# A norm, a gate and the order of weight splits rearranged at the seams of a two-layer transformer

## The chip, the core and the metric

The program runs on one core of a Trainium2 chip. The metric is the device time of one execution in microseconds. TensorE multiplies matrices into PSUM, VectorE and ScalarE do elementwise work, GpSimd does a few odd operations, and the SyncE queue issues the loads. Each engine works through its own queue of instructions; where one needs the result of another, it waits.

## The reference

Two layers over 512 tokens of width 1024, all in fp32. Each layer mixes tokens, then runs a gated feed-forward block (hidden width 2816), each with a norm before and after and a residual.

```python
for layer in range(DEPTH):
    a = rmsnorm(h, ln_mix_pre[layer])
    mem_n = rmsnorm(mem, ln_mem[layer])
    if layer < N_A_LAYERS:
        proj = a @ w_in_a[layer]
        u, v, q_mem = ...
        main = chunked_spatial_gating(u, v, w_spatial[layer], ...)
    else:
        s_in = rmsnorm(h, ln_shared)
        kvf = s_in @ w_shared_kv
        k_s, v_s = ...
        log_f_s = jax.nn.log_sigmoid(kvf[..., 2 * MAIN_WIDTH:] + b_forget)
        proj = a @ w_in_b[layer - N_A_LAYERS]
        q, q_mem = ...
        main = forgetting_attention(q, k_s, v_s, log_f_s)
    mixed = jnp.concatenate([main, memory_attention(q_mem, mem_n, w_mem_kv[layer])], axis=-1)
    h = h + rmsnorm(mixed @ w_out[layer], ln_mix_post[layer])
    f = rmsnorm(h, ln_ffn_pre[layer])
    f = (jax.nn.silu(f @ w_ffn_gate[layer]) * (f @ w_ffn_up[layer])) @ w_ffn_down[layer]
    h = h + rmsnorm(f, ln_ffn_post[layer])
```

`forgetting_attention` adds the cumulative sum of `log_f_s` along the tokens to its logits, for twelve heads. `memory_attention` has four heads over 256 memory rows.

## The kernel before

**Numbers.** Every fp32 operand is cut into a high part, rounded by a ScalarE copy, and a low part, the rest, which VectorE subtracts (`split`, L240). A product is three matmuls (`mm3`, L191): high by high, high by low, low by high. A pair of weight parts lives in the tiles `whi` and `wlo`, eight buffers each. TensorE can start on `whi` as soon as ScalarE is done, and needs `wlo` at the third matmul.

**Stages.** Layer A: memory queries, value projection, memory heads, spatial gating. Then a feed-forward block, layer B (queries, keys, values, forget gates, four memory heads, twelve forgetting heads), and a second feed-forward block. Between them stands `boundary` (L835) three times: it finishes the tail of the one stage, transposes its rows into the hidden state `h`, adds up the squares for the next norm (`PairNorm`, L301) and runs the first four blocks of the next stage in halves of 256 tokens.

**Norms.** `finish` (L275) sums squares by a matmul against a column of 1/1024, one for each 128 tokens and each summed tile; `spread` (L292) lays the result over all partitions by `broadcast` (L249).

**The feed-forward block.** Hidden blocks are taken two at a time for the gate and the up projection. One such block of 256 hidden columns is a `Seven` (L921): seven products of twelve matmuls each, from sums of the quarters of the weight block, and from sums of the inputs made once (`combined`). `sums` (L940) makes the first sums (`s3` and some in place in `raw`) and splits the first two weights; `run` splits the others on their turn; `end` (L979) adds the seven results up into `s1` and `s2`, for which it reads PSUM after the last product (`a`), and hands the rows on to `gate_rows` (multiply by the norm `rbc`, then SiLU) or `up_rows` (multiply by the gate, then split into `fhi` and `flo`). The PSUM tiles of a Seven are `x`, `a` and `e`. `sevens` (L988) runs a gate Seven and an up Seven. For the first pair of a block it mixes the two; for the nine other pairs it runs them one after the other, products in the order 1, 7, 2, 6, 4, 3, 5. There are 20 Sevens in a block; after 6, 12 and 16 of them a down projection follows, and behind the last the tail. In this document Sevens are numbered as in the rows: odd ones are gates, even ones ups.

**What sets the order.** The code is written stage by stage, and a scheduler places each instruction in its engine's queue as its own estimates of readiness say, so that the queue of an engine can run ahead of the written order. `tc.issue_after(ins)` keeps instructions behind a given one on the same engine; it adds no wait between engines. Once built, the queues are fixed. Where stages meet, pieces of one stage are handed to another to fill TensorE (`fill`, `take`, `attend`).

**Forget gates.** Layer B loads the twelve columns `w_f`, splits them into one stationary tile of 24 columns and runs sixteen matmuls against the 512 tokens (L1185), turns the result with four transposes (L1190), and computes the log-sigmoid in small steps on VectorE and ScalarE (`az`, `e`, `l1`, `lf`). After six pieces of the value and key blocks it forms the cumulative sum with eight matmuls (`cs`, L1223). Only then do the memory heads start.

Of the kernel before, what the change touches and what calls it, by code (L numbers as in the profile page):

```python
# [40 lines left out]
def hybrid(ctx: ExitStack, tc: tile.TileContext, i: dict, out: bass.AP):  # L41
# [10 lines left out]
    last_load, last_exp = [None], [None]  # L52
# [80 lines left out]
    def pair_of_parts(n=512, aside=False):  # L133
        if aside:
            return act("whi"), act("wlo")
        return (wp.tile([P, 512], F32R, tag="hi", name=name("whi"), bufs=8)[:, :n],
                wp.tile([P, 512], F32R, tag="lo", name=name("wlo"), bufs=8)[:, :n])
# [102 lines left out]
    def split(src, hi, lo, eng=None):  # L240
        A.copy(hi, src)  # L241
        (eng or V).tensor_sub(lo, src, hi)  # L242

    def scaled_parts(src, g, hi, lo):

        A.activation(hi, src, AF.Copy, scale=g)
        V.scalar_tensor_tensor(out=lo, in0=src, scalar=g, in1=hi, op0=ALU.mult, op1=ALU.subtract)

    def broadcast(r4, tbs, o, c0):  # L249

        for tb in tbs:
            PE.matmul(o[:, tb * P - c0 : (tb + 1) * P - c0], r4[:, tb : tb + 1].to_broadcast([P, P]),
                      ident, start=True, stop=True)
# [47 lines left out]
    class PairNorm(Norm):  # L301
# [255 lines left out]
    def layer_a():  # L557
        a = parts("a")
        pre = Norm()
        wq, raws = ([], []), [wp.tile([P, 1024], F32, tag="raw", name=name("raw"), bufs=4) for _ in range(2)]  # L560
# [21 lines left out]
        vg = {}  # L582

        def value_block(j):

            w, o = [], []

            def load():
                for kh in range(2):
                    w.extend(prepared(i["w_a_v"][j, kh], (4, 256)))  # L590

            def piece(tk, kh):
                if kh == 0:
                    o.append(ps("mm", (P, 256), s="v"))
                c = slice(tk * P, (tk + 1) * P)
                for k in range(4 * kh, 4 * kh + 4):
                    mm3(o[tk], (a[k][0][:, c], a[k][1][:, c]), w[k], k == 0, k == KT - 1)
                if kh:
                    if tk % 2 == 0:
                        vg[j, tk // 2] = plain("vg", (P, 2, 256))  # L600
                    A.activation(vg[j, tk // 2][:, tk % 2, :], o[tk], AF.Copy, scale=pre.r4[:, tk : tk + 1])

            return load, [lambda tk=tk, kh=kh: piece(tk, kh) for tk in range(TB) for kh in range(2)]

        with tc.tile_pool(name="sgu", bufs=1) as lp:
# [8 lines left out]
            for f in take(fill, 1):  # L614
                f()
# [5 lines left out]
            for f in take(fill, 1):  # L621
                f()
            for cols in HALVES:
                pre.spread(cols, rbc)
# [4 lines left out]
            for f in take(fill, 3):  # L629
                f()  # L630
            xs = mem_inputs(0, memt)
            wk = mem_key_weights(0)
            for f in take(fill, 2):
                f()
            norm.finish((0, NMEM))
            for f in take(fill, 1):
                f()
# [197 lines left out]
    def boundary(phase, post, pre, nnorm, dst, block, evac, scaled=None):  # L835
# [5 lines left out]
        tail, ys = phase  # L841
        h0, h1 = HALVES
# [27 lines left out]
        for tb in range(3):  # L870
            tail(tb)
        turn(0, range(2))
# [48 lines left out]
    class Seven:  # L921
# [57 lines left out]
        def end(self):  # L979
            left, right = (slice(*c) for c in HALVES)  # L980
            s1, s2 = self.s1, self.s2
            V.tensor_add(s2[:, left], self.q, s2[:, left])
            V.tensor_add(s2[:, right], self.p, s2[:, right])  # L983
            self.rows(1, s2)
            V.tensor_add(s1, self.x, s1)
# [112 lines left out]
    def layer_b(phase, fp):  # L1098
# [51 lines left out]

        def value_block(j):

            w, o = [], []

            def load():
                for kh in range(2):
                    w.extend(prepared(i["w_v"][j, kh], (4, 256)))

            def piece(tk, kh):
                if kh == 0:  # L1160
                    o.append(ps("mm", (P, 256), s="v"))
# [3 lines left out]
                if kh:  # L1165
                    if tk % 2 == 0:
                        vals[j, tk // 2] = plain("vf", (P, 2, 256))
                    V.tensor_scalar_mul(vals[j, tk // 2][:, tk % 2, :], o[tk], r4b[:, tk : tk + 1])
# [5 lines left out]


        wf = wp.tile([P, KT, HEADS], F32, tag="wf", name="wf", bufs=1)
        wfs = wp.tile([P, KT, 2, HEADS], F32R, tag="wfs", name="wfs", bufs=1)
        later([(wf, i["w_f"])])
        split(wf, wfs[:, :, 0, :], wfs[:, :, 1, :])
        o = ps("mm", s="f")  # L1180
        n2 = 2 * HEADS
        for k in range(KT):
            w = wfs[:, k, :, :].rearrange("p a b -> p (a b)")
            for x in range(2):
                PE.matmul(o[:n2, :], w, s_act[k][x], start=(k, x) == (0, 0), stop=(k, x) == (KT - 1, 1))  # L1185
        zr = plain("zr")
        V.tensor_copy(zr[:n2, :], o[:n2, :])
        zt = ps("tr", (P, TB, 2, HEADS), s="zt")
        for tb in range(TB):
            PE.transpose(zt[:, tb, :, :].rearrange("p a b -> p (a b)"), zr[:n2, tb * P : (tb + 1) * P], ident[:n2, :n2])  # L1190
        bf = cp.tile([P, HEADS], F32, name="bf")
        later([(bf, i["b_f"].partition_broadcast(P))])

        def fsmall(s, dt=F32):
            return sp.tile([P, TB, HEADS], dt, tag="fs", name=name(s), bufs=10)

        z, zs = fsmall("z"), fsmall("zs")
        V.tensor_copy(zs, zt[:, :, 1, :])
        V.tensor_add(zs, zt[:, :, 0, :], zs)
        for tb in range(TB):  # L1200
            V.scalar_tensor_tensor(out=z[:, tb, :], in0=zs[:, tb, :], scalar=r4b[:, tb : tb + 1], in1=bf,
                                   op0=ALU.mult, op1=ALU.add)
        az, e, w1, l1, c1_ = fsmall("az"), fsmall("e"), fsmall("w1"), fsmall("l1"), fsmall("c1")
        A.activation(az, z, AF.Abs)
        A.activation(e, az, AF.Exp, scale=-1.0)

        V.tensor_scalar_add(w1, e, 1.0)
        A.activation(l1, w1, AF.Ln)
        V.scalar_tensor_tensor(out=c1_, in0=w1, scalar=-1.0, in1=e, op0=ALU.add, op1=ALU.subtract)
        V.reciprocal(w1, w1)  # L1210
        V.tensor_mul(c1_, c1_, w1)
        V.tensor_sub(l1, l1, c1_)
        lf = fsmall("lf")
        V.scalar_tensor_tensor(out=lf, in0=z, scalar=0.0, in1=l1, op0=ALU.min, op1=ALU.subtract)
        lfh, lfl = fsmall("lfh", F32R), fsmall("lfl", F32R)
        split(lf, lfh, lfl)
        for f in take(fill, 6):
            f()
        cs = ps("mm", s="cs")
        for tb in range(TB):  # L1220
            n = T - tb * P
            for part in (lfh, lfl):
                PE.matmul(cs[:HEADS, tb * P :], part[:, tb, :], tri[:, :n],  # L1223
                          start=(tb == 0 and part is lfh), stop=(tb == TB - 1 and part is lfl))
        cc = tp.tile([P, T], F32R, tag="acc", name="cc", bufs=2)
        ch, cl, nh, nl = (cc[32 * n : 32 * n + HEADS, :] for n in range(4))
        A.copy(ch, cs[:HEADS, :])
        V.tensor_sub(cl, cs[:HEADS, :], ch)
        A.activation(nh, ch, AF.Copy, scale=-1.0)
        V.tensor_sub(nl, ch, cs[:HEADS, :])  # L1230
# [13 lines left out]
        def head_parts(u, n):  # L1244
# [6 lines left out]
            for dst, src in ((qa[own, :], qh), (qa[other, :], ql), (ka[own, :], kh), (ka[other, :], kh),  # L1251
                             (qc[:64, :], qh), (kc[:64, :], kl)):
                nc.sync.dma_start(dst.bitcast(F32), src[own, :].bitcast(F32))
            nc.sync.dma_start(qc[66:68, :].bitcast(F32), cc[n : n + 33 : 32, :].bitcast(F32))
# [19 lines left out]
        between = {n: take(fill, c) for n, c in enumerate((3, 3, 4, 4, 4, 4, 4, 4, 3, 3, 3, 3))}  # L1274
# [103 lines left out]
```

## Time and profile before

| what | us |
|---|---|
| median of three timed runs (lowest, highest) | 1131.23 (1130.92, 1131.71) |
| span of the profiled execution | 1130.7 |
| TensorE busy | 1116.5 |
| weight loads busy | 1015.8 |
| VectorE busy | 893.1 |
| ScalarE busy | 662.2 |

The profile is one execution on the chip; the times in its rows count from the start of its span, and no separate device time stands for it beside the span. A row of the groups gives line, engine, operation, output<-inputs, shape and count, then busy time, mean ns of one, and the idle time ahead with what ended it. A row of the timeline gives start, duration, engine, line, operation, and in brackets the idle time ahead with what ended it; `x4` merges four neighbours. Matmuls are pipelined, so the sum of durations is more than the time between starts.

### The profile page before, as it was taken

The numbers are of one execution on the slowest core, as the hardware profiler recorded it, in microseconds if no ns is written. First come the engines' busy times: TensorE is split into PE (matmuls) and PEld (weight loads), VectorE is DVE, ScalarE is ACT, GpSimd is POOL, SyncE is SP. The second block draws the span as 40 slices with busy tenths as digits, with TensorE's granted clock in tenths as the row PEclk, the third lists the DMA queues.
The fourth block names the chain that finished last, engine by engine and source line by source line (L and its number), as shares of the span: only waits on it lengthen the run. The fifth ranks groups of instructions, "written<-read, shape, count | busy, mean of one in ns | idle before, by whom it ended". The sixth has DMA issues, their size and how long they took to land.

```text
span 1130.7 us, 19666 instructions
## 1 busy us (share of the span) xinstructions
PE 1116.5 (99%) x7470; PEld 1015.8 (90%) x7471; DVE 893.1 (79%) x1717; ACT 662.2 (59%) x1385; POOL 24.7 (2%) x42
## 2 busy tenths in 40 slices
PE   9999999999999999999999999999999999999997
PEld 6998889999899898998988898889999899898995
DVE  7878558897698587796858889958998688588775
ACT  8774468664365264476637667768765266254453
POOL 1000000000000000000000000000000000000000
PEclk9999999999999999999999999999999999999999
DMA  7513222334134223343323455521224234133222
GB/s 262 159 38 113 89 79 76 112 111 132 57 112 149 64 87 112 98 152 107 96 93 90 112 128 135 137 75 57 68 102 150 75 104 135 62 112 113 75 75 75
DMA packets 63559, 118.14 MB, mean 104 GB/s; under 512 B 5164, under 2 KB 39992, under 8 KB 63464
## 3 DMA queue, kind: packets, MB, share of 16 engines
q1 hardware_dynamic: 62584, 116.05, 33.1%
q8 instruction: 59, 0.97, 0.3%
q0 software_dynamic: 192, 0.52, 0.2%
q10 hardware_dynamic: 688, 0.31, 0.1%
q14 instruction: 36, 0.29, 0.1%
HBM read 104.71 MB, written 2.10 MB: 94 GB/s over the span
## 4 chain that ended last, share of the span: by engine, by line
PE 88%; DVE 4%; ACT 3%; issue 2%; DMA 2%; POOL 1%; SPq 0%; POOLq 0%; DVEq 0%
PE y L195 9%; PE y L194 9%; PE y L193 9%; PE a L195 5%; PE a L194 5%; PE a L193 5%; PE ps L193 4%; PE ps L195 4%; PE ps L194 4%; PE e L193 3%; PE e L195 3%; PE e L194 3%; PE x L195 3%; PE x L194 3%; PE x L193 3%
## 5 line engine op out<-in xcount | busy, mean ns | idle before, releaser
L241 ACT CAST whi<-raw 128x512 fp32r<-128x512 f32 x460 | 276.7, 620 | 271.4 <-PE y L195 111.3
L242 DVE TENSOR_TENSOR wlo<-raw,whi 128x512 fp32r<-128x512 f32 x460 | 305.6, 685 | 113.2 <-ACT whi L241 109.2
L193 PE MATMUL y<-whi,fhi 128*128 128x512 f32 (+1 forms) x356 | 138.5, 390 | 0.9 <-DVE s L983 0.6
L194 PE MATMUL y<-wlo,fhi 128*128 128x512 f32 (+1 forms) x356 | 138.0, 388 | 0.3 <-DVE wlo L242 0.3
L195 PE MATMUL y<-whi,flo 128*128 128x512 f32 (+1 forms) x356 | 138.1, 388 | 0.1
L193 PE MATMUL x<-xshi,whi 128*128 128x256 f32 x320 | 90.6, 283 | 0.0
L194 PE MATMUL x<-xslo,whi 128*128 128x256 f32 x320 | 90.6, 283 | 0.0
L195 PE MATMUL x<-xshi,wlo 128*128 128x256 f32 x320 | 90.6, 283 | 0.0
L194 PE MATMUL a<-xslo,whi 128*128 128x256 f32 x320 | 90.5, 283 | 0.0
L193 PE MATMUL a<-xshi,whi 128*128 128x256 f32 x320 | 90.5, 283 | 0.0
L195 PE MATMUL a<-xshi,wlo 128*128 128x256 f32 x320 | 90.4, 283 | 0.0
L193 PEld LDWEIGHTS y<-whi,fhi 128*128 128x128 f32 x356 | 66.9, 188 | 15.4 <-DVE s L983 1.3
L195 PEld LDWEIGHTS y<-whi,flo 128*128 128x128 f32 x356 | 66.9, 188 | 14.6 <-DVE flo L242 1.1
L194 PEld LDWEIGHTS y<-wlo,fhi 128*128 128x128 f32 x356 | 66.9, 188 | 14.3 <-DVE wlo L242 1.2
L193 PE MATMUL ps<-xshi,whi 128*128 128x256 f32 (+1 forms) x224 | 67.8, 305 | 0.0
L195 PE MATMUL ps<-xshi,wlo 128*128 128x256 f32 (+1 forms) x224 | 66.8, 300 | 0.0
L194 PE MATMUL ps<-xslo,whi 128*128 128x256 f32 (+1 forms) x224 | 66.2, 298 | 0.0
L193 PEld LDWEIGHTS a<-xshi,whi 128*128 128x128 f32 x320 | 61.4, 192 | 0.3
L194 PEld LDWEIGHTS a<-xslo,whi 128*128 128x128 f32 x320 | 61.4, 192 | 0.3
L193 PEld LDWEIGHTS x<-xshi,whi 128*128 128x128 f32 x320 | 61.4, 192 | 0.0
L194 PEld LDWEIGHTS x<-xslo,whi 128*128 128x128 f32 x320 | 61.4, 192 | 0.0
L195 PEld LDWEIGHTS x<-xshi,wlo 128*128 128x128 f32 x320 | 61.4, 192 | 0.0
(292 smaller groups left out, 3115.6 us busy)
## 6 DMA issues: line engine op xcount, KB each, us to landing
raw<-in_w_gate SPq DMA_DIRECT2D x44, 512.0 KB, 4.2
raw<-in_w_up SPq DMA_DIRECT2D x44, 512.0 KB, 3.5
raw<-in_w_down SPq DMA_DIRECT2D x44, 512.0 KB, 3.7
raw<-in_w_out SPq DMA_DIRECT2D x16, 512.0 KB, 4.7
raw<-in_w_b_q SPq DMA_DIRECT2D x8, 512.0 KB, 3.5
raw<-in_w_a_v SPq DMA_DIRECT2D x6, 512.0 KB, 6.4
raw<-in_w_a_u SPq DMA_DIRECT2D x6, 512.0 KB
raw<-in_w_v SPq DMA_DIRECT2D x6, 512.0 KB, 3.4
```

Source lines behind the costliest of these rows:

```text
L193: PE.matmul(o, w[0], x[0], start=start, stop=False, skip_group_check=more)
L194: PE.matmul(o, w[0], x[1], start=False, stop=False, skip_group_check=more)
L195: return PE.matmul(o, w[1], x[0], start=False, stop=stop, skip_group_check=more)
L241: A.copy(hi, src)
L242: (eng or V).tensor_sub(lo, src, hi)
```

## The change

It does these things. (1) `sevens` puts what `sums` issues on VectorE behind the last addition of the previous Seven. (2) `PairNorm` adds its two halves on VectorE and gives one tile to the sum by matmul instead of two. (3) `broadcast` uses a transpose instead of a matmul. (4) Layer A computes the squares of its norm behind the last split of its inputs, finishes the norm once for all tokens after three pieces of the value blocks, and holds back the copies of finished value pieces until the norm is there. (5) `boundary` puts the splits of the next stage's weights behind the first tail's, delays the last block by 3 steps instead of 4, and finishes the first half's norm after step 6. (6) The forget gates become twelve more columns of layer B's first value block: its weight tiles are 268 columns wide, and `z` is read from those columns. The log-sigmoid and the cumulative sum become pieces between the memory heads, which start without them; the counts of pieces between heads change to match.

```diff
+    @contextmanager
+    def behind(some):
+        with ExitStack() as s:
+            for ins in some:
+                s.enter_context(tc.issue_after(ins.ins))
+            yield
...
-            PE.matmul(o[:, tb * P - c0 : (tb + 1) * P - c0], r4[:, tb : tb + 1].to_broadcast([P, P]),
-                      ident, start=True, stop=True)
+            PE.transpose(o[:, tb * P - c0 : (tb + 1) * P - c0], r4[:, tb : tb + 1].to_broadcast([P, P]), ident)
...
+            t = self.sq[0, cols]
             if j:
-                V.tensor_add(self.sq[0, cols], self.sq[0, cols], self.sq[j, cols])
+                V.tensor_add(t, t, self.sq[j, cols])
+            if j == KT // 2 - 1:
+                V.tensor_add(t[:, 0, :], t[:, 0, :], t[:, 1, :])
         def sums(self, tb, cols):
-            c = slice(tb * P - cols[0], (tb + 1) * P - cols[0])
-            return [self.sq[0, cols][:, x, c] for x in range(2)]
+            return [self.sq[0, cols][:, 0, tb * P - cols[0] : (tb + 1) * P - cols[0]]]
...
-            for k in range(KT):
-                pre.add(h[:, k, :])
-            for cols in HALVES:
-                pre.finish(cols)
+            with behind(last_a):
+                for k in range(KT):
+                    pre.add(h[:, k, :])
+            pieces(3)
+            pre.finish(FULL)
+            pre.done = True
...
-        ws = [block(n) for n in range(4)]
-        outs = group(ws, inputs(0), h0, ["mm", "lg"] * 2, lag=4,
-                     after={3: lambda: turn(1, range(2)), 5: lambda: turn(1, range(2, 4))})
-        nnorm.finish(h0)
+        with behind(phase_parts):
+            ws = [block(n) for n in range(4)]
+        outs = group(ws, inputs(0), h0, ["mm", "lg"] * 2, lag=3,
+                     after={3: lambda: turn(1, range(2)), 5: lambda: turn(1, range(2, 4)),
+                            6: lambda: nnorm.finish(h0)})
...
-            V.tensor_add(s1, self.x, s1)
+            end = V.tensor_add(s1, self.x, s1)
             self.rows(0, s1)
+            ended[0] = end
+    ended = [None]
     def sevens(pair, plain_first):
         if not plain_first:
             for make in pair:
                 u = make()
-                u.sums()
+                with behind(ended):
+                    u.sums()
...
+            width = 256 + (0 if j else HEADS)
...
+                    raw = loaded(i["w_v"][j, kh]).rearrange("p (a b) -> p a b", b=256)
+                    for x in range(0, 4, 2):
+                        pair = [t.rearrange("p (a b) -> p a b", a=2) for t in pair_of_parts(2 * width)]
+                        k = 4 * kh + x
+                        split(raw[:, x : x + 2, :], *(t[:, :, :256] for t in pair))
+                        split(wf[:, k : k + 2, :], *(t[:, :, 256:] for t in pair))
...
+                    if j == 0:
+                        V.scalar_tensor_tensor(out=z[:, tk, :], in0=o[tk][:, 256:], scalar=r4b[:, tk : tk + 1], in1=bf,
+                                               op0=ALU.mult, op1=ALU.add)
...
-        split(wf, wfs[:, :, 0, :], wfs[:, :, 1, :])
-        o = ps("mm", s="f")
-        for k in range(KT):
-            w = wfs[:, k, :, :].rearrange("p a b -> p (a b)")
-            for x in range(2):
-                PE.matmul(o[:n2, :], w, s_act[k][x], start=(k, x) == (0, 0), stop=(k, x) == (KT - 1, 1))
...
-        between = {n: take(fill, c) for n, c in enumerate((3, 3, 4, 4, 4, 4, 4, 4, 3, 3, 3, 3))}
+        between = {n: take(fill, c) for n, c in enumerate((5, 5, 5, 5, 4, 4, 4, 4, 3, 3, 3, 3))}
+        between[1].insert(4, forget)
+        between[2].insert(3, cumulate)
```

The queues change most inside the feed-forward blocks. First VectorE around the end of Seven 7, in the first feed-forward block. In the rows the first number of a name counts the tile (`s2_7` is of Seven 7, `wlo_128` to `wlo_134` are the low parts of Seven 8, `wlo_135` and `wlo_136` of Seven 9), the second is a buffer number. Before:

```order
L982 TENSOR_TENSOR s2_7_3582<-e_7_3580,s2_7_3582 128x256
L242 TENSOR_TENSOR wlo_133_3809<-raw_53_3711,whi_133_3808 128x512
L242 TENSOR_TENSOR wlo_134_3825<-raw_54_3713,whi_134_3824 128x512
L242 TENSOR_TENSOR wlo_135_3866<-raw_55_3854,whi_135_3865 128x512
L983 TENSOR_TENSOR s2_7_3582<-a_7_3579,s2_7_3582 128x256
L985 TENSOR_TENSOR s1_7_3581<-x_7_3578,s1_7_3581 128x512
L1032 TENSOR_TENSOR s2_7_3582<-s2_7_3582,rbc_115 128x512
L1032 TENSOR_TENSOR s1_7_3581<-s1_7_3581,rbc_115 128x512
L242 TENSOR_TENSOR wlo_136_3871<-raw_55_3854,whi_136_3870 128x512
```

And with the change:

```order
L999 TENSOR_TENSOR s2_7_3574<-e_7_3572,s2_7_3574 128x256
L1000 TENSOR_TENSOR s2_7_3574<-a_7_3571,s2_7_3574 128x256
L1002 TENSOR_TENSOR s1_7_3573<-x_7_3570,s1_7_3573 128x512
L1053 TENSOR_TENSOR s2_7_3574<-s2_7_3574,rbc_115 128x512
L1053 TENSOR_TENSOR s1_7_3573<-s1_7_3573,rbc_115 128x512
L961 TENSOR_TENSOR s3_8_3712<-raw_53_3703,raw_54_3705 128x512
L241 TENSOR_TENSOR wlo_128_3715<-raw_53_3703,whi_128_3714 128x512
L963 TENSOR_TENSOR raw_54_3705<-raw_54_3705 128x512
L241 TENSOR_TENSOR wlo_129_3720<-raw_53_3703,whi_129_3719 128x512
L965 TENSOR_TENSOR raw_53_3703<-raw_54_3705,raw_53_3703 128x512
L241 TENSOR_TENSOR wlo_130_3739<-s3_8_3712,whi_130_3738 128x512
```

Before, all low parts of Seven 8 and the first of Seven 9 stood ahead of the addition `s2_7<-a_7`, which reads Seven 7's last product. Now that addition and the four instructions that follow from it stand ahead of Seven 8's first sum `s3_8` and its first low part `wlo_128`.

Second, TensorE where Seven 8 hands over to Seven 9. Before:

```order
L193 MATMUL a_8_3716<-xshi_6_2125,whi_134_3824 128x256
L194 MATMUL a_8_3716<-xslo_6_2126,whi_134_3824 128x256
L195 MATMUL a_8_3716<-xshi_6_2125,wlo_134_3825 128x256
L193 MATMUL a_9_3859<-xshi_1_1926,whi_135_3865 128x256
L194 MATMUL a_9_3859<-xslo_1_1927,whi_135_3865 128x256
L195 MATMUL a_9_3859<-xshi_1_1926,wlo_135_3866 128x256
```

And with the change:

```order
L193 MATMUL a_8_3708<-xshi_6_2132,whi_134_3816 128x256
L194 MATMUL a_8_3708<-xslo_6_2133,whi_134_3816 128x256
L195 MATMUL a_8_3708<-xshi_6_2132,wlo_134_3817 128x256
L193 MATMUL a_9_3851<-xshi_1_1920,whi_135_3857 128x256
L194 MATMUL a_9_3851<-xslo_1_1921,whi_135_3857 128x256
L193 MATMUL e_9_3852<-t3hi_1_2396,whi_137_3881 128x256
L195 MATMUL a_9_3851<-xshi_1_1920,wlo_135_3858 128x256
```

The first product of Seven 9 starts as before with the two matmuls on `whi_135`; one matmul of its second product (`e_9`) has moved ahead of the first one that needs `wlo_135`.

Third, ScalarE in layer B, around the forget gates (`az`, `e`, `l1`, `lfh`) and the memory heads' softmax (`mp`). Before:

```order
L1204 ACTIVATE az_1_6945<-z_1_6937 128x48
L1205 ACT_TABLE_LOAD
L1205 ACTIVATE e_21_6946<-az_1_6945 128x48
L1208 ACT_TABLE_LOAD
L1208 ACTIVATE l1_1_6948<-w1_1_6947 128x48
L241 CAST lfh_1_6960<-lf_1_6958 128x48
L241 CAST vals0_6872<-vf_1_7009 128x4x64
L241 CAST vals1_6873<-vf_1_7009 128x4x64
L1227 CAST cc_7083<-cs_1_7074 12x512
L1229 ACTIVATE cc_7083<-cc_7083 12x512
L432 ACT_TABLE_LOAD
L432 ACTIVATE mp_9_7128,sm_5_7097<-mlg_17_7129,nmx_5_7096 128x256
```

And with the change:

```order
L440 ACTIVATE mp_12_7135,sm_6_6912<-mlg_24_7158,nmx_6_6911 128x256
L1220 ACTIVATE az_1_7180<-z_1_6900 128x48
L241 CAST vals1_6863<-vf_2_7102 128x4x64
L1221 ACTIVATE e_21_7181<-az_1_7180 128x48
L241 CAST whi_283_7353<-q_11_6112 128x512
L1224 ACT_TABLE_LOAD
L1224 ACTIVATE l1_1_7183<-w1_1_7182 128x48
L241 CAST pT_21_7216<-tr_11_7215 128x512
L440 ACT_TABLE_LOAD
L440 ACTIVATE mp_13_7224,sm_7_6914<-mlg_25_7225,nmx_7_6913 128x256
```

Before, the chain and its table loads stood ahead of the first memory head's exponential (`mp_9`). Now two memory heads' exponentials come first, the chain stands between `mp_12` and `mp_13`, and two table loads with it.

More of the change, by code (lines that the diff above doesn't have):

```diff
@@ L1 @@
-from contextlib import ExitStack
+from contextlib import ExitStack, contextmanager
 import concourse.bass as bass
@@ L135, in pair_of_parts @@
             return act("whi"), act("wlo")
-        return (wp.tile([P, 512], F32R, tag="hi", name=name("whi"), bufs=8)[:, :n],
-                wp.tile([P, 512], F32R, tag="lo", name=name("wlo"), bufs=8)[:, :n])
+        return (wp.tile([P, max(n, 512)], F32R, tag="hi", name=name("whi"), bufs=8)[:, :n],
+                wp.tile([P, max(n, 512)], F32R, tag="lo", name=name("wlo"), bufs=8)[:, :n])
     def cut(pair, w):
@@ L559, in layer_a @@
         pre = Norm()
+        pre.done = False
         wq, raws = ([], []), [wp.tile([P, 1024], F32, tag="raw", name=name("raw"), bufs=4) for _ in range(2)]
@@ L613, in layer_a, with pieces @@
                         idle(2, zero, end)
-            for f in take(fill, 1):
-                f()
-            for k in range(KT):
-                pre.add(h[:, k, :])
-            for cols in HALVES:
-                pre.finish(cols)
+            def pieces(n):
+                for f in take(fill, n):
+                    f()
+            with behind(last_a):
[4 more added lines that the diff above has]
+            pre.done = True
             memt = load_mem()
[L621 to L624, printed above, removed]
+            pieces(1)
+            pre.spread(FULL, rbc)
             qf = [plain("q") for _ in range(2)]
@@ L628, in layer_a @@
             norm = mem_sums(memt)
-            for f in take(fill, 3):
-                f()
+            pieces(1)
             xs = mem_inputs(0, memt)
             wk = mem_key_weights(0)
-            for f in take(fill, 2):
-                f()
             norm.finish((0, NMEM))
-            for f in take(fill, 1):
-                f()
+            pieces(3)
             norm.spread((0, NMEM), rmem)
@@ L1186, in layer_b @@
[L1186 to L1228, printed above, removed]
@@ L1229, in layer_b, with forget @@
-        A.activation(nh, ch, AF.Copy, scale=-1.0)
-        V.tensor_sub(nl, ch, cs[:HEADS, :])
+        def forget():
+            az, e, w1, l1, c1_ = fsmall("az"), fsmall("e"), fsmall("w1"), fsmall("l1"), fsmall("c1")
+            A.activation(az, z, AF.Abs)
+            A.activation(e, az, AF.Exp, scale=-1.0)
+            V.tensor_scalar_add(w1, e, 1.0)
+            A.activation(l1, w1, AF.Ln)
+            V.scalar_tensor_tensor(out=c1_, in0=w1, scalar=-1.0, in1=e, op0=ALU.add, op1=ALU.subtract)
+            V.reciprocal(w1, w1)
+            V.tensor_mul(c1_, c1_, w1)
+            V.tensor_sub(l1, l1, c1_)
+            lf = fsmall("lf")
+            V.scalar_tensor_tensor(out=lf, in0=z, scalar=0.0, in1=l1, op0=ALU.min, op1=ALU.subtract)
+            sums["parts"] = fsmall("lfh", F32R), fsmall("lfl", F32R)
+            split(lf, *sums["parts"])
@@ new lines, in cumulate @@
+        def cumulate():
+            cs = ps("mm", s="cs")
+            lfh, lfl = sums["parts"]
+            for tb in range(TB):
+                n = T - tb * P
+                for part in (lfh, lfl):
+                    PE.matmul(cs[:HEADS, tb * P :], part[:, tb, :], tri[:, :n],
+                              start=(tb == 0 and part is lfh), stop=(tb == TB - 1 and part is lfl))
+            cc = sums["cc"] = tp.tile([P, T], F32R, tag="acc", name="cc", bufs=2)
+            ch, cl, nh, nl = (cc[32 * n : 32 * n + HEADS, :] for n in range(4))
+            A.copy(ch, cs[:HEADS, :])
+            V.tensor_sub(cl, cs[:HEADS, :], ch)
+            A.activation(nh, ch, AF.Copy, scale=-1.0)
+            V.tensor_sub(nl, ch, cs[:HEADS, :])
```

45 lines of the change are left out of this document (29 added, 16 removed).

## The prediction

> **What bounds the kernel now.** I read the busy shares first, then the chain that ended last, then the engines' waits, then one stretch of feed-forward work row by row.
>
> ```profile
> PE 1116.5 (99%) x7470; PEld 1015.8 (90%) x7471; DVE 893.1 (79%) x1717; ACT 662.2 (59%) x1385; POOL 24.7 (2%) x42
> ...
> PE 88%; DVE 4%; ACT 3%; issue 2%; DMA 2%; POOL 1%; SPq 0%; POOLq 0%; DVEq 0%
> ```
>
> TensorE is busy for 1116.5 of 1130.7 us and carries 88% of the chain: what leaves TensorE's queue is gained in full, and what makes it wait is lost in full. VectorE's 79% is an average; in the feed-forward blocks it looks different:
>
> ```profile
> 320.00:340.00 20.00, 20.00 (x169) 20.00 (x168) 19.17 (x34) 12.62 (x26) 0.00 (x0) 1.00 0.32 106
> ```
>
> Columns are the stretch, its length, then busy time of PE, PEld, DVE, ACT and POOL, granted clock and DMA. In these 20 us TensorE never stops and VectorE is busy for 19.17. Two engines run side by side, each with about as much work as there is time. That holds only while VectorE prepares the next Seven's weights during the present Seven's products. An edit that puts the two one behind the other shows at once.
>
> **The change part by part.** The diff has three kinds of edits, and they pull in opposite directions.
>
> *Less work on TensorE.* Four stretches give the prices:
>
> ```profile
> 183.50 0.95 PE L284 MATMUL st<-avg,sq 128*128 128x1 f32 x8
> 184.32 0.36 PE L193 MATMUL ps<-xshi,whi 128*128 128x256 f32 x1
> ...
> 185.86 0.71 PE L252 MATMUL rb<-ident,r 128*128 128x128 f32 x4
> 186.33 0.36 PE L195 MATMUL ps<-xshi,wlo 128*128 128x256 f32 x1
> ```
>
> Four norm sums leave eight records and hold the queue from 183.50 to 184.32, 0.82 us. At the three boundaries each half now sends two sums instead of four: six times 0.41, 2.5 us. Two broadcasts leave four records and hold it from 185.86 to 186.33, 0.47 us, two records each; as transposes I count one record each, which is how the attention's transposes stand in the groups (64 records for 64 tiles):
>
> ```profile
> L448 PE MATMUL tr<-ident,mp 128*128 128x128 f32 x64 | 9.1, 272 | 0.0
> ```
>
> Half of 0.47, for ten pairs of broadcasts: 2.4 us. [...]
>
> ```profile
> 584.92 0.40 PE L1185 MATMUL f<-shi,wfs 128*24 128x512 f32 x1
> ...
> 588.61 0.28 PE L193 MATMUL v<-whi,shi 128*128 128x256 f32 x1
> ...
> 589.65 0.42 PE L1190 MATMUL zt<-ident,zr 24*128 24x24 f32 x4
> 590.00 0.39 PE L195 MATMUL v<-whi,slo 128*128 128x256 f32 x1
> ```
>
> The forget gates' sixteen matmuls hold the queue for 3.69 us and their four transposes for 0.35. Against them stand twelve more columns in 96 matmuls. From 0.23 us between starts at 512 columns (rows L1185) and 0.12 at 256 (rows at 309 us, below), a column costs 0.43 ns: 96 x 12 x 0.43 ns = 0.5 us. Net 3.5 us. Together the three leave TensorE 8.4 us less.
>
> *Moves around seams.* Layer A's squares go behind the splits of its inputs, its norm is finished once, boundaries run with lag 3 and finish after step 6, and the forget chain goes between memory heads. What could be won is bounded by TensorE's waits at such places, of which the largest are
>
> ```profile
> PE yt L799 <- ACT y L792: 1.4, 3, 0.6
> PE idle L88 <- DVE zeros L80: 1.3, 1, 1.3
> PE mlg L465 <- ACT mp L432: 1.0, 1, 1.0
> PE rb L252 <- POOL r L256: 0.9, 2, 0.7
> ```
>
> (total, times, longest). Some 2 us of it (rb and mlg) is in reach. What could be lost is two ACT table loads, now between softmaxes of the second and third memory head:
>
> ```profile
> L1208 ACT ACT_TABLE_LOAD x1 | 1.3, 1283 | 0.0
> ```
>
> twice 1.28 us, with key-block matmuls on TensorE as cover; without it up to 2.6 us. I take these moves at 0, with ends of -2 and +3 us. New VectorE adds for the norms (six of 256 columns, 0.33 us apart at the boundaries) stay off TensorE's path, since they replace sums that come later anyway.
>
> *The order inside the Sevens.* This is the large term. `sums()` of a Seven is put behind the previous Seven's last addition on VectorE. VectorE takes its queue in order. The previous Seven's end needs its last product; the next Seven's first product needs, at its third matmul, `wlo`, which now stands behind that end. Before, `wlo` was written a whole Seven earlier. So TensorE and VectorE wait for each other once per Seven. The rows for the price, first the hand-over:
>
> ```profile
> 309.06 0.28 PE L195 MATMUL e<-t,wlo 128*128 128x256 f32 x1
> 309.18 0.28 PE L193 MATMUL x<-xshi,whi 128*128 128x256 f32 x1
> ...
> 309.45 0.42 DVE L982 TENSOR_TENSOR s<-e,s 128x256 f32<-128x256 f32 x1 [0.24 <-PE e L195]
> ```
>
> Matmuls start 0.12 us apart; the last one ends 0.28 after its start; VectorE begins 0.11 after that end. Call that end E. Then VectorE's pitch:
>
> ```profile
> 323.49 0.42 DVE L983 TENSOR_TENSOR s<-a,s 128x256 f32<-128x256 f32 x1
> 323.82 0.68 DVE L985 TENSOR_TENSOR s<-x,s 128x512 f32<-128x512 f32 x1
> 324.42 0.68 DVE L1038 SCALAR_TENSOR_TENSOR s<-s,s 128x512 f32<-128x512 f32 x1
> 325.02 0.68 DVE L1040 TENSOR_TENSOR s<-s,s 128x512 f32<-128x512 f32 x1
> 325.62 0.68 DVE L242 TENSOR_TENSOR wlo<-raw,whi 128x512 fp32r<-128x512 f32 x1
> ```
>
> Starts are 0.60 to 0.61 apart at 512 columns, and each is done 0.68 after its start. ScalarE's copy, which `s1` needs, takes 0.37:
>
> ```profile
> 322.75 0.37 ACT L971 COPY s<-a 128x256 f32<-128x256 f32 x1
> ```
>
> Gate to up: `s2` at E+0.11, `s1` after the copy at E+0.51, two products with `rbc` at 1.12 and 1.72, the sum `s3` at 2.33, `wlo` at 2.93, done at 3.62. With 0.10 for the hand-over to TensorE (a guess of mine near the 0.11 above), the third matmul starts at E+3.72 instead of E+0.08: a wait of 3.64. The second product's third matmul comes twelve matmuls (1.44) later, at 5.16, but its `wlo` stands four instructions on, done at 6.04, started at 6.14: 0.98 more. After that each product (1.44) outlasts one or two instructions of VectorE. Together 4.62 us.
>
> Up to gate: five instructions of 512 columns stand ahead of `wlo` instead of four (`flo` of the hidden block is among them), so it is done at E+4.22; the first wait is 4.12. Then five more stand ahead of the second product's `wlo`, done at 7.25, with thirteen matmuls of cover: 1.47. Together 5.59 us.
>
> How often: each layer has Sevens 1 to 20. The first two overlap as before, and 7, 13 and 17 begin behind a down projection, whose matmuls cover the preparation. Fifteen hand-overs are bare in a layer, nine gate to up and six up to gate, thirty in the kernel. One of them, ahead of Seven 19 in the first layer, also has eight memory inputs between its low parts:
>
> ```profile
> 27.36 2.46 DVE L247 SCALAR_TENSOR_TENSOR mparts<-mem,gains,mparts 128x256 fp32r<-128x256 f32 x6
> ```
>
> 0.41 each, 3.3 us, of which some 2.1 shows. 18 x 4.62 + 12 x 5.59 + 2.1 = 152.3 us.
>
> *Sum.* 1130.7 - 8.4 + 152.3 = 1274.6 us of span; the median run, 1131.23, stands 0.5 above the profiled span, so 1275.
>
> **The rivals.** *The clock falls in the gaps.* So far no wait is above 1.3 us, and the granted clock is 1.00 throughout. The gaps would be 3.6 and 4.1 us, thirty times. The trace shows TensorE after an idle start:
>
> ```profile
> 6.52 0.50 PE L194 MATMUL ps<-alo,whi 128*128 128x512 f32 x1 [0.29 <-DVE alo L247]
> ...
> 7.55 0.50 PE L193 MATMUL ps<-ahi,whi 128*128 128x512 f32 x1
> 7.89 0.40 PE L194 MATMUL ps<-alo,whi 128*128 128x512 f32 x1
> 8.27 0.50 PE L195 MATMUL ps<-ahi,wlo 128*128 128x512 f32 x1
> ...
> 9.87 0.39 PE L195 MATMUL ps<-ahi,wlo 128*128 128x512 f32 x1
> 10.10 0.40 PE L193 MATMUL ps<-ahi,whi 128*128 128x512 f32 x1
> ```
>
> After the last wait that the view notes, at 6.52, matmuls start 0.34 to 0.38 us apart, and from 9.87 on 0.23: a slow spell of 3.4 us. A spell of that length at half pace loses 1.7 us; about 1.0 of it is covered, since the slow first product hides the second wait. That leaves 0.7 us for each of thirty gaps; a spell twice as long would leave 2.4. So 1296 to 1347, in the middle 1320. [...]
>
> *Only the first wait shows.* If ScalarE and VectorE regain the second product's parts in the first gap, the 0.98 and 1.47 fall away: 35 us less, 1240. Against it: VectorE's rows have no idle time in between to regain.
>
> *Faster after all.* The end of a Seven would have to reach VectorE before TensorE needs the low part, which takes 3.7 us of matmuls after E that need no low part, thirty of them; the new order has two or three (0.24 to 0.36). If the queue order were not kept on the chip, the sum would be 1130.7 - 8.4 + 0.5: 1123. The trace of before keeps the built order row for row there, so I give this little.
>
> **How the numbers follow.** Forecast 1275: 0.67. Clock rival 0.20, first wait alone 0.08, faster 0.04, no difference 0.01 (within 0.2%, about what a measurement can tell here). The hand-over, 0.11 either way for sixty waits, and the moves at -2 and +3 bound the forecast's own range to 1262 to 1290. The range given, 1250 to 1325, reaches up to the middle of the clock rival; it leaves out that rival's upper part (0.06) and the cases below (0.13).
>
> **What would show it.** VectorE: `s<-a` of L1000 idle behind PE at each Seven, then `wlo` late; TensorE: waits of some 3.7 and 1 us on `wlo` of DVE, in total about 150, all in the feed-forward slices; its busy time down by about 8 us if the clock holds, and 256-column matmuls 0.12 apart right after a gap. If they stand 0.24 apart there, the clock rival holds. If layer B's forget term is wrong, its stretch is not 3 us shorter. The forecast is wrong if VectorE's wait at the end of a Seven is short.

## The result, and the profile after

The changed kernel takes 1313.41 us (median of four runs, 1311.67 to 1315.5) beside 1131.31 us for the kernel before: a ratio of 1.161, 95% interval 1.159 to 1.162. The time lies in the range given, 38 us above the predicted one. The first lines of the page of after, with the line of the granted clock, PEclk (one digit for each fortieth of the span, in tenths of TensorE's full clock):

```profile
span 1310.1 us, 19297 instructions
PE 1183.6 (90%) x7408; PEld 1066.3 (81%) x7409; DVE 891.4 (68%) x1721; ACT 660.7 (50%) x1388; POOL 25.4 (2%) x41
PEclk9999999789888989979999999999889889979989
```

TensorE has 62 matmul records fewer than before and is busy 67 us longer; it now also stands still for some 126 us. A smaller amount of work that takes longer means that it ran slower: the clock line is not all nines any more, and the mean granted clock fell from 0.999 to 0.937. In the trace it stands at 1.00 or at 0.50. At 0.50 for a share s of the span the mean is 1 - s/2, so s is 12.6%, some 165 us.

Where TensorE waits (total us, times, longest), and where VectorE does:

```profile
PE a L195 <- DVE wlo L241: 66.9, 21, 3.7
PE e L193 <- ACT whi L241: 45.6, 12, 4.1
PE e L195 <- DVE wlo L241: 2.0, 4, 0.6
PE x L195 <- DVE wlo L241: 1.8, 1, 1.8
```

```profile
DVE s L999 <- PE e L195: 138.2, 38, 6.2
DVE s L1000 <- ACT s L988: 83.5, 33, 2.8
```

Three of the 21 waits on `wlo` last 0.17 us; the other 18 are the gate-to-up hand-overs. The 12 in the second row are those from up to gate, where TensorE waits for the `whi` of the second product, which ScalarE copies from VectorE's sum `s3`. Together 30 long waits, 112 us. VectorE in turn waits 222 us at the end of a Seven for its last products (L999) and for ScalarE's copy of the last one (L1000), at places where it worked on the next weights before. At each bare hand-over the two engines now wait for each other.

One hand-over in order of time (start, duration, engine, instruction, idle time before it), on VectorE and on TensorE:

```profile
338.18 0.42 DVE L1000 TENSOR_TENSOR s<-a,s 128x256 f32<-128x256 f32 x1 [2.77 <-ACT s L988]
338.52 0.68 DVE L1002 TENSOR_TENSOR s<-x,s 128x512 f32<-128x512 f32 x1
339.11 1.28 DVE L1053 TENSOR_TENSOR s<-s,rbc 128x512 f32<-128x512 f32 x2
340.31 0.69 DVE L961 TENSOR_TENSOR s<-raw,raw 128x512 f32<-128x512 f32 x1
340.92 0.68 DVE L241 TENSOR_TENSOR wlo<-raw,whi 128x512 fp32r<-128x512 f32 x1
```

```profile
337.69 0.28 PE L194 MATMUL a<-xslo,whi 128*128 128x256 f32 x1
341.66 0.58 PE L195 MATMUL a<-xshi,wlo 128*128 128x256 f32 x1 [3.69 <-DVE wlo L241]
...
343.32 0.42 PE L193 MATMUL a<-xshi,whi 128*128 128x256 f32 x1
343.53 0.41 PE L194 MATMUL a<-xslo,whi 128*128 128x256 f32 x1
...
348.16 0.28 PE L194 MATMUL x<-xslo,whi 128*128 128x256 f32 x1
348.28 0.28 PE L195 MATMUL x<-xshi,wlo 128*128 128x256 f32 x1
```

VectorE runs through exactly the instructions that the prediction counted, and the wait is 3.69 us. It starts on them later than counted: `s<-a` (L1000) comes behind ScalarE's copy of the same product, 0.45 us after that product's end at 337.73, where the prediction had 0.11. What follows is the new part: matmuls start 0.21 us apart, and only from 347.5 on 0.12.

### The profile page after: what moved, and what is told of

It is laid out like the page before. It is cut to its first block, busy times and chain, and to the rows that moved or that the text cites. A ratio compares the mean times of both kernels' runs of the same rounds, so it can differ in the third digit from the quotient of the medians.

```text
span 1310.1 us, 19297 instructions
## 1 busy us (share of the span) xinstructions
PE 1183.6 (90%) x7408; PEld 1066.3 (81%) x7409; DVE 891.4 (68%) x1721; ACT 660.7 (50%) x1388; POOL 25.4 (2%) x41
## 4 chain that ended last, share of the span: by engine, by line
PE 78%; DVE 13%; ACT 5%; issue 3%; DMA 1%; POOL 1%; SPq 0%; POOLq 0%; DVEq 0%; ACTq 0%
PE y L193 8%; PE y L194 8%; PE y L195 8%; PE a L195 5%; PE a L193 4%; PE a L194 4%; PE e L195 4%; PE e L193 4%; PE e L194 3%; PE x L193 3%; PE x L195 3%; PE x L194 3%; PE ps L195 3%; PE ps L193 3%; PE ps L194 3%
## 5 line engine op out<-in xcount | busy, mean ns | idle before, releaser
L195 PE MATMUL a<-xshi,wlo 128*128 128x256 f32 x320 | 107.9, 337 | 66.9 <-DVE wlo L241 66.9
L195 PEld LDWEIGHTS a<-xshi,wlo 128*128 128x128 f32 x320 | 73.3, 229 | 73.5 <-DVE wlo L241 73.5
L999 DVE TENSOR_TENSOR s<-e,s 128x256 f32<-128x256 f32 x40 | 17.0, 424 | 138.2 <-PE e L195 138.2
L194 PE MATMUL a<-xslo,whi 128*128 128x256 f32 x320 | 100.2, 313 | 0.0
L193 PE MATMUL e<-t3hi,whi 128*128 128x256 f32 x160 | 58.9, 368 | 45.6 <-ACT whi L241 45.6
L193 PE MATMUL a<-xshi,whi 128*128 128x256 f32 x320 | 100.0, 312 | 0.0
L193 PEld LDWEIGHTS e<-t3hi,whi 128*128 128x128 f32 x160 | 43.5, 272 | 48.1 <-ACT whi L241 48.1
L988 ACT COPY s<-a 128x256 f32<-128x256 f32 x40 | 14.8, 370 | 117.6 <-PE a L195 117.6
L1000 DVE TENSOR_TENSOR s<-a,s 128x256 f32<-128x256 f32 x40 | 16.9, 423 | 83.5 <-ACT s L988 83.5
L194 PEld LDWEIGHTS a<-xslo,whi 128*128 128x128 f32 x320 | 70.9, 222 | 0.3
```

The source lines that it names most:

```text
L193: PE.matmul(o, w[0], x[0], start=start, stop=False, skip_group_check=more)
L194: PE.matmul(o, w[0], x[1], start=False, stop=False, skip_group_check=more)
L195: return PE.matmul(o, w[1], x[0], start=False, stop=stop, skip_group_check=more)
L988: A.copy(s1[:, right], self.p)
```

## The experiments

**One edit undone, and that edit alone.** The first kernel takes the order inside the Sevens back and keeps the rest of the change; the second adds only that order to the kernel before.

```diff
-                with behind(ended):
-                    u.sums()
+                u.sums()
```

> The changed kernel with one edit taken back: sums() of a Seven is no longer put behind the previous Seven's last addition; all other edits stay. Theory (the order inside the Sevens is the whole loss): the thirty waits on wlo and the half clock go with it; granted clock 1.00, and the time is 1131.3 - 8.4 = 1123 us, 1120 to 1126 with the moves at -2 and +3. Rival (the other edits lose too, at the seams or in layer B): 1131 us or more, with new waits of TensorE outside the feed-forward blocks.

> The kernel before with that one edit alone: sums() behind the previous Seven's last addition. Theory: the whole loss stands here again, 1313.4 - 1123 = 190 us over the kernel before, so 1322 us, 1316 to 1327, with a mean granted clock near 0.94 and thirty waits of 3.7 us. Rival (part of the loss needs the other edits beside it): under 1310 us. The forecast as it was made, without a fall of the clock: 1131.3 + 152.3 = 1284 us.

Measured: 1123.19 us without it, ratio to before 0.9928 (0.9916 to 0.9941), and 1329.12 us with it alone, ratio 1.174 (1.173 to 1.176). A line of the page of the first, and the waits of the second:

```profile
PE 1108.6 (99%) x7409; PEld 1003.3 (89%) x7409; DVE 893.2 (80%) x1721; ACT 659.4 (59%) x1388; POOL 25.4 (2%) x41
```

```profile
PE a L195 <- DVE wlo L242: 66.5, 19, 3.7
PE e L193 <- ACT whi L241: 45.5, 12, 4.1
```

The whole loss is this one edit; all others together are a gain. Alone it costs 198 us, 8 more than within the change (190), outside what was expected: the waits are the same to 0.5 us, but the mean clock is 0.927 and not 0.937. The gaps lie elsewhere in time there, and more of that kernel runs at half clock.

**The gaps filled.** The next kernel separates waiting from the clock. It adds matmuls that nobody reads, behind the last product before each of the thirty bare hand-overs:

```diff
                 u = make()
+                if end_mm[0] is not None:
+                    idle(12, tri, end_mm[0])
                 with behind(ended):
```

> The changed kernel with twelve more matmuls of 512 columns, whose result nobody reads, behind the last product before each of the thirty bare hand-overs: 12 x 0.23 = 2.8 us of work in a gap of 3.7 us. Theory (of the loss, 112 us are the first waits and some 71 us are matmuls at half clock after the gaps): the clock stays at 1.00, TensorE starts at full pace after each gap, and now waits for the second product as forecast, 0.98 or 1.47 us: 1270 to 1280 us, with more work in the kernel than the changed one. Rival (the matmuls after a gap are slow for a reason other than the gap, such as VectorE working beside them): 1313 us or more. Rival (the second wait doesn't come): near 1240 us.

Measured: 1254.66 us (1253.94 to 1255.15). More work, and 59 us less time: that is the price of the half clock, as far as the filling changes nothing else. Its waits, and the start of a Seven behind the filling:

```profile
PE a L195 <- DVE wlo L241: 17.1, 18, 1.0
PE e L193 <- ACT whi L241: 12.8, 12, 1.4
PE x L195 <- DVE wlo L241: 3.3, 1, 3.3
```

```profile
330.22 2.89 PE L88 MATMUL idle<-tri 128*128 128x512 f32 x12
332.95 0.28 PE L193 MATMUL a<-xshi,whi 128*128 128x256 f32 x1
333.07 0.28 PE L194 MATMUL a<-xslo,whi 128*128 128x256 f32 x1
334.31 0.38 PE L195 MATMUL a<-xshi,wlo 128*128 128x256 f32 x1 [0.96 <-DVE wlo L241]
334.53 0.28 PE L193 MATMUL a<-xshi,whi 128*128 128x256 f32 x1
...
335.81 0.28 PE L193 MATMUL x<-xshi,whi 128*128 128x256 f32 x1
...
336.76 0.33 PE L195 MATMUL e<-t3hi,wlo 128*128 128x256 f32 x1
```

The filling takes 2.7 us and 0.96 is left to wait: the same hand-over of 3.7 us, now at full clock (one gap of the thirty still ends in slow matmuls, 0.41 us each from 234.11 to 237.10), and VectorE works beside the matmuls as in the changed kernel: from 320 to 380 us it is busy for 37.9 us at a granted clock of 1.00, there for 32.9 at 0.86. So here it is the gap that makes them slow, not VectorE's work beside them. The time is below the 1270 to 1280 expected, since the second wait hardly shows: in this kernel's order TensorE does eight matmuls of `x` between the parts of `e` that need no low part and the one that does (335.81 to 336.76).

**How much idle time the clock stands.** Two more kernels fill each gap with six and with eight matmuls.

> The changed kernel with six filling matmuls in each of the thirty gaps in place of twelve: 1.4 us of work, so that some 2.3 us of each gap stay idle, and no stretch of 3.41 us is without a matmul. Theory (the clock is set on a grid of 3.41 us; it falls after a stretch in which TensorE was busy for less than about 1.6 us, whatever the idle time was made of): an idle run of 2.3 us brings a stretch under 1.6 us when it lies so on the grid that 1.8 us of it or more fall into one stretch, in some 60% of places; so about 18 of 30 gaps end at half clock, at some 2 us each: 1255 + 36 = 1290 us, 1270 to 1305. Rival (a whole stretch must be idle): no fall of the clock, 1255 us.

> The same with eight: 1.84 us of work, some 1.85 us idle. Theory: hardly any place on the grid puts 1.8 us of idle time into one stretch; the clock falls after a few gaps at most: 1255 to 1262 us. Rival (the length of the idle run alone decides, as a share of the gap): between the run with six and that with twelve, 1272 us.

Measured: 1274.74 us (1270.76 to 1276.16) and 1268.7 us (1266.13 to 1270.23). With six fillers 17 gaps end at half clock where 18 were expected; the time is in the expected range, but 15 us below its middle, since one such gap costs (1274.74 - 1254.66) / 17 = 1.2 us and not 2. For eight I was wrong: 14 gaps still do, 14 us over the filled kernel. The error was in the arithmetic: an idle run of some 1.87 us that falls into one stretch of 3.41 us whole leaves 1.54 us busy, as in the first pair with eight below, which ends at half clock; by these lengths I estimate that it falls so in (3.41 - 1.87) / 3.41, about 45% of places, not in hardly any. Stretches between the steps at which the granted clock changed (busy time of TensorE, granted clock), first one pair with six fillers, then two with eight:

```profile
334.22:337.63 3.41, 1.09 (x9) 1.00 0.00 0
337.63:341.05 3.42, 3.42 (x18) 0.50 0.00 0
```

```profile
526.64:530.05 3.41, 1.54 (x13) 1.00 0.00 0
530.05:533.47 3.42, 3.42 (x18) 0.50 0.00 0
345.73:349.14 3.41, 1.68 (x9) 1.00 0.01 2
349.14:352.56 3.42, 3.08 (x21) 1.00 0.02 5
```

**The release earlier.** Here `ended` is the previous Seven's first addition, of product 4, in place of the last:

```diff
-            V.tensor_add(s2[:, left], self.q, s2[:, left])
+            end = V.tensor_add(s2[:, left], self.q, s2[:, left])
...
-            end = V.tensor_add(s1, self.x, s1)
+            V.tensor_add(s1, self.x, s1)
```

> The changed kernel with sums() behind the previous Seven's first addition (of product 4) in place of its last (of product 5): the release comes 24 matmuls, 2.8 us, earlier, and the five instructions that the next first product needs stand ahead of the last additions. Theory (the loss is set by the instructions of VectorE that stand between the last product and the next low part): the first wait goes; the low part of s3 is now done 4.0 us after the last product (gate to up) or 4.6 (up to gate), and 28 matmuls (3.3 us) stand ahead of its use: 18 x 0.7 + 12 x 1.3 = 28 us over 1123, 1151 us, 1135 to 1160; no gap is over 1.5 us and the clock stays at 1.00. Rival (any order behind the neighbour's end breaks the overlap): over 1200 us. Rival (the cover suffices): 1123 to 1130.

Measured: 1175.07 us (1174.6 to 1176.16), ratio 1.039 (1.037 to 1.040). The first wait is gone but for the first hand-over of each block (1.2 and 1.5 us left), and so is nearly all of the half clock (mean clock 0.994), and with them 138 of 190 us; but the run is 24 us above what was expected.

```profile
PE e L195 <- DVE wlo L241: 16.9, 19, 1.2
PE x L193 <- ACT whi L241: 8.4, 10, 0.9
PE y L193 <- DVE s L1000: 5.1, 4, 1.8
```

The wait on the low part of `s3` is there about as worked out, 0.8 us from gate to up (expected 0.7) and 1.0 from up to gate (expected 1.3). What was left out is ScalarE: after an up Seven it casts the hidden block (`fhi`, twice 0.62 us) before `whi` of the next product, so `x` waits for ScalarE where VectorE alone was counted. And the down projections now wait for the late end of the Seven before them. These rows make 30 of the 52 us over 1123; the rest are waits and restarts shorter than a row each, which I did not sort out.

**The small edits, one taken back at a time,** from the kernel at 1123.19 us.

> The kernel without the order inside the Sevens (1123.2 us), and with the forget gates back as sixteen matmuls of their own. Theory (each of the three savings is what it was priced at): 3.5 us more, 1126.7. Rival (the twelve columns cost what the sixteen matmuls did, or the pieces between memory heads cost a table load or two): 1123 or less.

> The same kernel (1123.2 us) with the halved norm sums and the transposed broadcasts taken back. Theory: 2.5 + 2.4 = 4.9 us more, 1128.1. Rival (the ones were hidden at the seams): 1123 to 1125.

> The same kernel (1123.2 us) with the moves at the start of layer A and at the boundaries taken back. Theory (priced at nothing): 1123, from 1120 to 1125. Rival (they win what TensorE waited for there): 1125 to 1127; rival (lag 3 and the deferred copies cost): 1119 to 1121.

Measured: 1126.07 us with the forget gates' own matmuls back, 1125.63 with the old norm sums and broadcasts, 1125.42 with the old seams; ratios to before 0.9946 (0.9933 to 0.9959), 0.9947 (0.9935 to 0.9959) and 0.9940 (0.9927 to 0.9952). Their intervals overlap with that of the kernel at 0.9928. So what these runs bear out is the sum, 8.1 us; the shares, 2.9, 2.4 and 2.2 us, are the best estimate. The forget term is near its 3.5, the norm term about half of its 4.9, and the seams, priced at nothing, look like a small gain rather than a loss.

**A version that beats both.** The kernel at 1123.19 us has one long wait left:

```profile
PE y L193 <- DVE s L1000: 2.6, 1, 2.6
```

It stands in the first layer's first down projection, where VectorE split weights that were still landing ahead of the sixth Seven's end.

```diff
                 for kp in range(nk // 2):
-                    w = down_weights(layer, k0 + 2 * kp, dh)
+                    with behind(ended if (layer, gi, dh) == (0, 0, 0) and kp == nk // 2 - 1 else []):
+                        w = down_weights(layer, k0 + 2 * kp, dh)
```

> The kernel without the order inside the Sevens (1123.2 us), with one order of the same kind put where it should help: in the first layer's first down projection, the last pair of weights of its first half is split behind the sixth Seven's last addition. In the 1123.2 us run that place has the only long wait left, 2.6 us of TensorE on that Seven's end, which stands on VectorE behind splits of weights that were still landing, and one stretch of 3.41 us at half clock after it. Theory: wait and half clock go, 2.6 + 1.7 = 4.3 us, 1119 us; 1118 to 1121. Rival (the splits put back are late in turn): 1122 to 1125.

Measured: 1121.85 us, ratio to before 0.9916 (0.9903 to 0.9930). The mean granted clock is 0.999, with a 9 in every slice of the page, but 1.8 us of the wait are left in two pieces:

```profile
PE y L193 <- DVE s L1000: 1.8, 2, 1.5
```

It is the fastest kernel of this study and faster than before; against 1123.19 its 1.3 us are within the intervals, and short of the 1119 expected.

## Why the prediction held, and where it failed

*Less work on TensorE: right as a sum.* 8.4 us forecast, 8.1 measured (6.7 to 9.5 from the interval), with the seams, put at nothing, inside it. By the best estimates the norm part was too large and the seams too small; the intervals don't separate them. One price in it was misread. The forecast halves the 0.47 us of a pair of broadcasts, by the count of records; in the changed kernel such a pair holds the queue for 0.14 us (from 645.67 to 645.81): some 70% off, not half. There are nine pairs (36 records before, 18 after) and not ten, and some held only 0.36 us before; all broadcasts together held the queue for 3.7 us and now for 1.4, so the 2.4 us is near the rows' 2.3 by luck.

*The order as the large term, its place and its count: right.* Thirty hand-overs, in the feed-forward slices alone, and the edit undone takes everything back.

*The first wait: right to some 5%.* 18 x 3.64 + 12 x 4.12 = 115 us forecast; the rows say 112, with 3.69 for gate to up and 3.7 (ten times) or 4.1 (twice) for up to gate. The rows count idle time from the end of the matmul before, the forecast from start to start. In its own measure the third matmul of the hand-over above starts at 341.66 instead of 337.81, 3.85 us late, and from up to gate it is some 4.3 us: by these two hand-overs an estimate of 121 us. The 0.2 us more each time come from VectorE's late start behind ScalarE's copy. From up to gate the gap also ends on another thing than the low part that was forecast: one matmul of the second product stands ahead, and waits for ScalarE's `whi`.

```profile
358.22 0.58 PE L193 MATMUL e<-t3hi,whi 128*128 128x256 f32 x1 [3.73 <-ACT whi L241]
358.77 0.58 PE L195 MATMUL a<-xshi,wlo 128*128 128x256 f32 x1
```

*The second wait: mis-sized.* The step "The second product's third matmul comes twelve matmuls (1.44) later" gave 35 us. In the changed kernel at most 3 us of such rows are left: the twelve matmuls run at half clock, take 2.6 us, and `wlo` of `s3` is done by then. At full clock with filled gaps, other matmuls were moved in between. Of the 131.5 us that the filled kernel loses against 1123.19, 112 are the filling (30 x 2.73) and the waits of its first two rows and 3.3 stand at Seven 19 (forecast 2.1, in the changed kernel 1.8), which leaves 16. Some 9 of these are the difference between start-to-start and the rows; the rest, second waits among them, was not sorted out.

*The clock: the step that failed.* The forecast held the clock at 1.00 and gave the rival 0.20. It fell after all thirty gaps. The filled kernel puts its price at 59 us, 2.0 for each gap; and the rows give about the same: the stretches at half clock hold some 620 matmul starts, each 0.213 - 0.118 = 0.095 us late, some 59 us. The rival's 1296 to 1347, in the middle 1320, holds the measured 1313, but its price was read from a stretch that doesn't show the clock: from 6.52 to 9.87 in the kernel before, the granted clock is 1.00, and among the matmuls stand pairs of fillers, which the shown rows leave out. The pair below takes 0.46 us up to the matmul at 7.55, full pace (0.23 each, as from 9.87 on):

```profile
7.09 0.61 PE L88 MATMUL idle<-zeros 128*128 128x512 bf16 x2
```

So the rival had the right mechanism, and its size by luck. The forecast went wrong in holding the clock through the gaps: that was an estimate of mine, which no run shows. In the changed kernel half clock followed all thirty, and most of the stretches ahead of it were not idle throughout. These are stretches of TensorE between the steps at which the granted clock changed there (stretch, length, busy, granted clock):

```profile
337.29:340.71 3.42, 0.67 (x6) 1.00 0.00 0
340.71:344.12 3.41, 2.46 (x11) 0.50 0.02 5
344.12:347.53 3.41, 3.41 (x18) 0.50 0.02 5
...
385.08:388.49 3.41, 1.71 (x15) 1.00 0.00 0
388.49:391.91 3.42, 1.22 (x8) 1.00 0.00 0
391.91:395.32 3.41, 2.88 (x15) 0.50 0.02 5
```

Here the stretches with 0.67 and 1.22 us of work are followed by half clock, and the one with 1.71 by full. Of the thirty stretches ahead of a fall behind a gap only three were without any matmul.

The trace of before held a hint, at the very end, where two transposes lie in a stretch that is otherwise idle:

```profile
1124.35:1127.76 3.41, 0.40 (x2) 1.00 0.71 197
1127.76:1130.70 2.94, 0.00 (x0) 0.50 0.03 8
```

It is no clean test: in the changed kernel the last stretch at full clock, 2.07 us busy from 1303.27 to 1306.68, most of it with transposes, was also followed by half clock, and no run here sets transposes apart from other matmuls.

So the sum is 1123.2 + 112 (first waits, by the rows) + 59 (clock) + 19 = 1313. The 19 is what is left over, the 3.3 at Seven 19 and the 16 of the filled kernel; it was not measured in the changed kernel by itself. The predicted 1275 is as near as it is by luck: a term that was too large, 35, stood where one was missing. The forecast's own range, 1262 to 1290, is also wider than its two terms give: sixty times 0.11 is 6.6 us, and with the moves that is 1266 to 1285.

## What to carry to other kernels

An order that puts the preparation of the next block behind the end of the present one turned two engines that ran side by side here into two that wait for each other; its price was the chain of instructions from that end to the first input needed (3.64 us counted and 3.69 measured from gate to up), and it can be counted from the rows before the kernel runs. Look for half clock behind the gaps that arise on TensorE as well: here it followed all thirty gaps of 3.7 to 4.1 us and added half as much again as the gaps themselves (59 us beside 112), and it still followed 17 of thirty with some 2.3 us idle and 14 of thirty with some 1.9. Before pricing what stands behind a first wait, read the built order on TensorE: what follows may be covered already.

## What the runs showed of the hardware

In the changed kernel the granted clock was 1.00 or 0.50, and each of the sixty spells between its first and its last record lasted 3.41 us or a whole multiple of that, up to 331.1. The steps lay differently from run to run: one at 340.71 us in the changed kernel, one at 337.63 with six fillers.

Taken from step to step, 3.41 us long, the stretches at full clock ahead of half clock, without the one at the very end, and those ahead of full clock had this much TensorE work:

| kernel | ahead of half clock (stretches) | ahead of full clock, least |
|---|---|---|
| changed | 0.00 to 1.31 us (30) | 1.61 us |
| the edit alone | 0.05 to 1.42 (30) | 1.78 |
| release earlier | 0.92 to 1.59 (3) | 1.71 |
| six fillers | 0.82 to 1.55 (17) | 1.59 |
| eight fillers | 0.93 to 1.64 (14) | 1.54 |

With twelve fillers the slow matmuls from 234.11 on (0.41 us each) stand behind a stretch from 230.55 that was busy, by its rows, for 1.94 us, more than any in the middle column; that one stays unexplained. Stretches at half clock that were followed by another had 1.65 to 3.02 us of work in the changed kernel (17), those followed by full clock 2.93 to 3.42 (30). Behind its thirty gaps of 3.7 to 4.1 us stood one stretch at half clock (14 times), two (15) or three (once). The edit alone and the edit within the change have the same waits to 0.5 us, yet 194 and 164 us of half clock by their mean clocks and spans. At the rate of the changed kernel, 59 us lost in 164, the 30 us more make an estimated 11 us, near the 8 between them.

In the changed kernel matmuls of 256 columns start 0.213 us apart at a granted clock of 0.50 and 0.118 at 1.00: a ratio of 1.8, not 2.

A transposed broadcast cost less here than the matmul that it replaced: a pair held TensorE's queue for 0.36 to 0.47 us as matmuls in the kernel before, and for 0.14 to 0.19 as transposes in the changed one (four at once, at 27.23, for 0.51; single ones for 0.03).
